# A two-layer backbone of four mixer groups on one core: the S5 group's TensorE steps given fixed places among the input projection's matmuls

## The chip, the cores and the metric

The kernel runs on one core of a Trainium2 chip, as one launch. The metric is device time in microseconds (us) of one execution; several executions are timed and the median is given. The core has five engines that run side by side, each through its own list of instructions in order: TensorE (PE, matmuls; PEld is its weight load), VectorE (DVE), ScalarE (ACT), GpSimd (POOL), and SyncE (SP), which issues DMA transfers. An instruction waits at the head of its engine's list until the data and buffers it needs are ready, and all behind it on that engine wait too.

## The reference

Two layers over 512 latent tokens and 256 context tokens, model width 2048. Each layer is one input projection that feeds four groups of heads, and one output projection:

```python
for l in range(DEPTH):                       # 2 layers
    z = modulated_rms_norm(x, c), modulated_rms_norm(ctx, c_ctx)
    s5, q, k, v, rkv, lora, hy, gate = split(z @ w_in[l])
    y_s5 = s5_mixer(s5, ...)                 # bidirectional complex state-space scan
    y_at = attn_mixer(q, k, v, ...)          # windowed attention with sink logits
    y_rw = rwkv_mixer(rkv, lora, ...)        # bidirectional RWKV-7 time mixing
    y_hy = hyena_seq(hy, ...)                # bidirectional order-2 long convolution
    y = concat(rms(y_s5), rms(y_at), y_rw, rms(y_hy))
    x = x + g * ((y * silu(gate)) @ w_out[l])

def s5_mixer(u):                             # 32 groups of 16 channels, 64 states, 2 directions
    h_t = lambda_bar * h_(t-1) + B_bar u_t   # associative scan, context first
    y = gelu(Re(C h) + d * u)
    return y * sigmoid(y @ glu_w + glu_b)
```

Layer 0 also produces the context's output; layer 1 needs only the latent one.

## The kernel before

**The input projection** is cut into tiles of 128 output columns. A tile takes its weights in four parts (loaded through `wr`, split into a high part `wh` on ACT, L1477, and a low part `wl` on DVE or POOL, L1478), and for each of 16 chunks of the input it runs three matmuls (L1638: high by high, high by low, low by high) 512 tokens wide, and three 256 wide where the context is computed. Three matmuls 512 wide are called a **unit** here, three 256 wide half a unit; a tile with the context is 24 units. L1535 and L1541 are matmuls of the next layer's modulation, which ride along with tiles.

**The order of a layer.** After the tile of the LORA columns come four tiles for S5 (`T_S5`), then the S5 group's own work; twelve tiles for RWKV (`T_R`); the RWKV group; then the projections of Q, K, V, of Hyena and of the gates, with attention, Hyena and the output projection (L1728) following. The code is written group by group, but a scheduler with a model of the engines decides at build time in which order the instructions of each engine stand. Matmuls of S5 so come to stand among those of the projection tiles that follow.

**S5** works on 16 batches (`batch`, four to each of four column tiles `tile`) in each layer. A tile loads u, transposes it twice on PE (L725, L733; evicted to `Uc` and `U`). A batch builds B on POOL and C on DVE and POOL (L768 to L779); `pk` is 16 small matmuls of C (L788), evicted to `kp`, written to memory and read back as the Toeplitz tile T by 16 transfers, whose two halves DVE adds (L805); `Bt` is four transposes (L811); `pv` is 16 matmuls of U (L831). From pv DVE and POOL make the state h (L833 to L849, scans at L839), and `py` is h by C (L855) and U by T (L857). A tile's readout transposes (L745) give y, which goes to memory; at the end comes the GLU over all four tiles (L880) and the group's rms norm, whose column sums are matmuls with ones at L134. After them the S5 buffers are given back, and the RWKV group's buffers take their place.

**RWKV** begins with features (L340 to L367, matmuls and transposes), which go by DMA to an inversion on POOL, L398 and L399 in turn; then a serial chain of steps (L446, L459, L439). Four columns by three blocks make 12 such blocks in a layer.

**Pace.** Units of the projections that run beside RWKV are held: a unit may not stand ahead of the RWKV step that its number asks for (`Pace`, with the first steps' allowance P0). These are order-only dependences: they fix who stands first in PE's list, and no engine waits on a semaphore for them.

**Milestones on PE.** Counted in units from the program's start, S5's first transposes of layer 0 stand at unit 67, its last norm matmuls at 317, the first feature matmul of RWKV at 360, the first chain step at 432, the third block's features at 474. In layer 1: 1296, 1494, 1524, 1604, 1638.

## Time and profile before

| | us |
|---|---|
| median of three runs | 3741.15 (3729.2 to 3751.39) |
| profiled execution | 3744.33 |
| its span | 3742.6 |
| PE busy in it | 3437.6 |
| DVE / ACT / POOL busy | 2169.5 / 1457.6 / 1305.2 |

The span is the time between the first and the last instruction on the core; the profiled execution's own time lies 1.7 us above it, and 3.2 us above the median. The mean granted TensorE clock is 0.942 of full speed. "Busy" counts matmuls and other work, not waiting. In rows of groups, "out<-in" names the tile written and those read.

### The profile page before, as it was taken

Reading aid. Unit: us, or ns where it says so; the run is one execution under the profiler, and the core shown is the slowest. Engines: PE = TensorE matmul, PEld = TensorE weight load, DVE = VectorE, ACT = ScalarE, POOL = GpSimd, SP = SyncE. Lnnn points to the kernel's source line nnn. Section 1 sums busy time; section 2 is a strip of 40 time slices with the busy share of each in tenths; the row PEclk is TensorE's granted clock in tenths of the full one; section 3 lists DMA queues with packets and bytes.
Section 4 is the critical chain, followed back from the end, with each engine's and each line's share of the span. In section 5 each row is a group of like instructions: output and inputs, shape, how many; then the busy total and the mean of one; then the engine's idle time right before and its main releaser. Section 6 shows DMA issues by size and latency. Waiting matters only on the chain. (4 is left out here: it accounts for less than half of the span.)

```text
span 3742.6 us, 63247 instructions
## 1 busy us (share of the span) xinstructions
PE 3437.6 (92%) x23478; PEld 2632.7 (70%) x23478; DVE 2169.5 (58%) x4011; ACT 1457.6 (39%) x2873; POOL 1305.2 (35%) x2328
## 2 busy tenths in 40 slices
PE   5998898999999999999999989778899989999999
PEld 1466676777777877787777776566776767677867
DVE  7675563546555553466668464754456565546765
ACT  3345443333433342345213454433334444435422
POOL 5654451244343432000144333631524355411031
PEclk9997999999999999999999989889998899899999
DMA  7854443644444444534533335444533334435244
GB/s 241 280 178 151 134 121 116 196 121 139 124 145 127 144 125 122 170 118 130 210 101 98 107 111 150 109 111 153 165 92 110 106 109 121 115 114 181 77 156 124
DMA packets 550608, 515.03 MB, mean 138 GB/s; under 512 B 166457, under 2 KB 396378, under 8 KB 549660
## 3 DMA queue, kind: packets, MB, share of 16 engines
q1 hardware_dynamic: 550300, 510.99, 45.0%
q8 instruction: 185, 3.03, 0.3%
q14 instruction: 123, 1.01, 0.1%
HBM read 404.40 MB, written 103.02 MB: 136 GB/s over the span
## 5 line engine op out<-in xcount | busy, mean ns | idle before, releaser
L1638 PE MATMUL pin<-hxh,wh 128*128 128x512 f32 (+1 forms) x2624 | 989.6, 377 | 19.6 <-ACT wh L1477 9.9
L1638 PE MATMUL pin<-hxh,wl 128*128 128x512 f32 (+1 forms) x2624 | 947.3, 364 | 9.6 <-POOL wl L1478 6.2
L1638 PE MATMUL pin<-hxl,wh 128*128 128x512 f32 (+1 forms) x2624 | 947.2, 362 | 0.0
L1477 ACT ACTIVATE wh<-wr 128x512 fp32r<-128x512 f32 x548 | 344.0, 629 | 861.0 <-PE pin L1638 426.9
L1638 PEld LDWEIGHTS pin<-hxh,wh 128*128 128x128 f32 x2624 | 507.7, 193 | 138.0 <-issue 34.3
L1638 PEld LDWEIGHTS pin<-hxh,wl 128*128 128x128 f32 x2624 | 506.5, 193 | 93.0 <-POOL wl L1478 8.5
L1638 PEld LDWEIGHTS pin<-hxl,wh 128*128 128x128 f32 x2624 | 508.7, 194 | 73.5 <-issue 5.6
L1478 DVE TENSOR_TENSOR wl<-wr,wh 128x512 fp32r<-128x512 f32 x434 | 319.4, 736 | 363.4 <-ACT wh L1477 345.4
L1478 POOL TENSOR_TENSOR wl<-wr,wh 128x512 fp32r<-128x512 f32 x114 | 155.0, 1360 | 927.0 <-ACT wh L1477 860.7
L398 POOL TENSOR_TENSOR rwtm<-rwAb,rwX 128x60 f32<-128x60 f32 (+24 forms) x744 | 257.7, 346 | 351.8 <-DMA rwAb<-rwAd 193.2
L399 POOL TENSOR_TENSOR rwX<-rwX,rwtm 128x60 f32<-128x60 f32 (+24 forms) x744 | 267.2, 359 | 57.2 <-DMA wr<-in_win 0.2
L1728 PE MATMUL pin<-yh,wl 128*128 128x512 f32 (+1 forms) x768 | 280.2, 366 | 5.7 <-DVE wl L1478 5.5
L1728 PE MATMUL pin<-yh,wh 128*128 128x512 f32 (+1 forms) x768 | 280.6, 367 | 2.9 <-ACT yh L1704 2.0
L1728 PE MATMUL pin<-yl,wh 128*128 128x512 f32 (+1 forms) x768 | 278.8, 363 | 2.2 <-DVE yl L1705 1.8
L1728 PEld LDWEIGHTS pin<-yh,wl 128*128 128x128 f32 x768 | 144.8, 189 | 32.1 <-DVE wl L1478 9.7
L1728 PEld LDWEIGHTS pin<-yh,wh 128*128 128x128 f32 x768 | 144.9, 189 | 28.8 <-ACT yh L1704 4.2
L1728 PEld LDWEIGHTS pin<-yl,wh 128*128 128x128 f32 x768 | 145.3, 189 | 25.8 <-DVE yl L1705 2.7
L1732 DVE SCALAR_TENSOR_TENSOR xt<-pin,GT,xt 128x512 f32<-128x512 f32 (+1 forms) x144 | 94.1, 656 | 95.7 <-PE pin L1728 95.3
L1535 PE MATMUL pin<-wr,cs 128*32 128x128 f32 x2048 | 115.9, 291 | 22.5 <-DMA wr<-in_wada 16.4
L448 ACT ACTIVATE rwKU<-mU 64x256 f32<-64x256 f32 x96 | 36.2, 377 | 173.9 <-PE mU L446 173.0
L405 ACT ACTIVATE rwXT<-rwXP 32x256 f32<-32x256 f32 x96 | 64.3, 670 | 81.6 <-DMA rwXP<-rwXd 80.1
L340 PE MATMUL mA<-rwZR,rwld 64*128 64x128 f32 x768 | 94.2, 292 | 1.4 <-DVE rwld L332 0.5
(606 smaller groups left out, 6204.6 us busy)
## 6 DMA issues: line engine op xcount, KB each, us to landing
wr<-in_win SPq DMA_DIRECT2D x408, 256.0 KB
wr<-in_wada SPq DMA_DIRECT2D x256, 256.0 KB
ada<-in_wada SPq DMA_DIRECT2D x64, 512.0 KB
wr<-in_wo SPq DMA_DIRECT2D x128, 256.0 KB
rwld<-rwF SPq DMA_DIRECT2D x20, 1024.0 KB
rwF<-ev SPq DMA_DIRECT2D x64, 256.0 KB
xt<-in_xin SPq DMA_DIRECT2D x32, 384.0 KB
rwLA<-ev SPq DMA_DIRECT2D x32, 384.0 KB
```

The costliest lines, as they stand in the source:

```text
L340: nc.tensor.matmul(pss[:, p, b, :], kb[hr, d * 2 + p, 2 * b:2 * b + 2, :].rearrange("p b s -> p (b s)"), ZR[hr, d, :, tt * 64:tt * 64 + 64 ...
L398: E.tensor_tensor(tm, Ab[:, 0:s, s:s + 1].to_broadcast([128, s, w]), X[:, s:s + 1, m:8].to_broadcast([128, s, w]), ALU.mult)
L399: E.tensor_tensor(X[:, 0:s, m:8], X[:, 0:s, m:8], tm, ALU.subtract)
L405: nc.scalar.activation(XT[r:r + 32, :, 32 * q:32 * q + 32].rearrange("p u (m g) -> p u m g", g=4), XR[r:r + 32].rearrange("p u (g m) -> p ...
L448: nc.scalar.activation(KU[rB, :, p, b, 1, :], up[rB].rearrange("p d a b -> p d (a b)"), AF.Copy, scale=-1.0)
L1477: nc.scalar.activation(h, raw, AF.Copy)
L1478: (nc.gpsimd if i % 4 == 3 else nc.vector).tensor_tensor(l, raw, h.bitcast(F32), ALU.subtract)
L1535: nc.tensor.matmul(ps[32 * j:32 * j + 32, :], self.cs[:, q * 4 + j, :], w3[:, j], start=q == 0, stop=q == 3, tile_position=(0, 32 * j))
L1638: mm.append(nc.tensor.matmul(ps, w[:, c], x[:, t], start=a, stop=b))
L1728: nc.tensor.matmul(ps, w[:, c], y[:, t], start=a, stop=b)
L1732: nc.vector.scalar_tensor_tensor(x[:, t], ps, self.GT[l][:, s, j:j + 1], x[:, t], ALU.mult, ALU.add)
```

## The change

A class `Weave` numbers the projection's units as they are issued, and takes S5's PE steps each with a place, in units. When it is closed, it lays a chain of order-only dependences through both lists: each step stands behind the last unit before its place, and each unit behind the last step before it. It covers the S5 tiles and the RWKV tiles of the projection (`T_S5`, `T_R`). With `S5AT` = (at, P), S5's first transposes stand at unit `at` of that count, batch pr has its place at b = at + 7 + pr·P: its B and C are issued for b − 1.05P, pk and Bt stand at b − 0.6P (batch 0 at `at` + 4), pv at b, py at b + 0.9P. A tile's transposes stand at 0.85P and 0.35P ahead of its first batch (tile 0 at `at` and `at` + 3), its readout 4.25P behind it.

So that code can be issued in that order, `tile` and `batch` become generators that name the place of their next piece, and `run` always takes the one with the lowest. U gets two buffers and the output columns `Yc` a tag of their own; small tiles share tags to make room. The GLU is issued last, as before, and is not given a place.

Line numbers shift: L1638 is L1699 after, L1535 L1596, L788 L833, L811 L856, L831 L878, L855 L904, L857 L906, L805 L850, L340 L374, L446 L480.

The diff, cut to its core:

```diff
+class Weave:
+    def unit(self, insts, w=1.0):
+        self.units.append((self.n, insts))
+        self.n += w
+    def step(self, at, insts):
+        self.steps.append((at, len(self.steps), insts))
+    def behind(self, insts, prev):
+        for i in insts:
+            self.tc.add_manual_dep(i.ins, prev.ins.name, mybir.DependencyInfo(mybir.DependencyClass.NoSync, mybir.DependencyReason.DATA), reason="weave")
+    def close(self):
+        self.steps.sort(key=lambda x: x[:2])
+        prev, step, q = None, None, list(self.steps)
+        for n, insts in self.units:
+            while q and q[0][0] <= n:
+                step = q.pop(0)[2]
+                if prev:
+                    self.behind(step, prev)
+                prev = step[-1]
+            if step:
+                self.behind(insts, step[-1])
+            prev = insts[-1]
...
 class S5:
...
+        yield b0 + (4 * ct - 0.85) * P if ct else self.at
...
-                nc.tensor.transpose(ps[0:96, i, :], u3[:, hf * 4 + i, :], idn)
+                self.lead(nc.tensor.transpose(ps[0:96, i, :], u3[:, hf * 4 + i, :], idn))
...
+        yield b0 + (4 * ct - 0.35) * P if ct else self.at + 3
-        U = t([128, 8, 128], "s5U")
+        U = t([128, 8, 128], "s5U", 2)
...
-        Yc = t([96, 8, 8, 16], "s5Uc")
-        for b in range(4):
-            self.batch(ct * 4 + b, U[:, b * 2:b * 2 + 2, :], Yc[:, :, b * 2:b * 2 + 2, :])
-        y = t([128, NT], "s5y")
+        Yc = self.Yc[ct] = t([96, 8, 8, 16], "s5Yc")
+        yield b0 + (4 * ct + 4.25) * P
+        y = t([128, NT], "s5u")
...
+    def lead(self, m):
+        self.weave.step(self.now, [m])
+
-    def batch(self, pr, U, Yc):
+    def batch(self, pr):
+        at, P = self.at + 7 + pr * self.per, self.per
+        yield at - 1.05 * P
...
+        yield at - 0.6 * P if pr else self.at + 4
         pk = k.bank("mA", 2, (128, 128))
...
+        yield at
         pv = k.bank("mU", 1, (128, 2, 2, 96))
...
+        yield at + 0.9 * P
         py = [k.bank("mY", 1, (128, 128))[0:96], k.bank("mI", 1, (128, 128))[0:96]]
...
     def run(self, srcs, outs, bg, eps):
         self.prepare()
-        for ct in range(4):
-            self.tile(ct, srcs[ct])
+        todo = [((b0 + (4 * ct - 2) * P, ct), self.tile(ct, srcs[ct])) for ct in range(4)]
+        todo += [((b0 + (pr - 1.06) * P, 4 + pr), self.batch(pr)) for pr in range(16)]
+        heap = {g: x for x, g in todo}
+        while heap:
+            g = min(heap, key=heap.get)
+            self.now = heap[g][0]
+            n = next(g, None)
...
         self.glu(outs, bg, eps)
...
                 if self.pace:
                     self.pace.unit(mm)
+                if self.weave:
+                    self.weave.unit(mm, (t.stop - t.start) / 512)
...
+S5AT = [(36, 19), (10, 17)]
```

What the two builds' lists hold. First PE, in layer 0, about one batch of S5 (mA takes pk and Bt, mU pv, mY and mI py). Before:

```order
L788 MATMUL mA_3547<-s5C_3538,s5BA_2770 32x128 x4
L788 MATMUL mA_3547<-s5C_3538,s5BB_2771 32x128 x2
L855 MATMUL mY_3515<-s5C_3428,s5h_3506 96x128
...
L855 MATMUL mI_3516<-s5C_3428,s5h_3506 96x128
L788 MATMUL mA_3547<-s5C_3538,s5BB_2771 32x128 x2
L811 MATMUL mA_3581<-c_ident,s5B_3529 128x128 x4
...
L857 MATMUL mY_3515<-s5T_3452,s5U_3294 96x128
...
L831 MATMUL mU_3598<-s5U_3294,s5Bt_3580 64x96 x8
L788 MATMUL mA_3657<-s5C_3648,s5BA_2770 32x128 x4
```

and after:

```order
L833 MATMUL mA_3645<-s5C_3607,s5BA_2770 32x128 x4
L833 MATMUL mA_3645<-s5C_3607,s5BB_2771 32x128 x4
L856 MATMUL mA_3679<-c_ident,s5B_3598 128x128 x4
L1596 MATMUL pin_5190<-wr_5307,cs 32x128 x4
L1699 MATMUL pin_5191<-hxh_1827,wh_5303 128x512
...
L1699 MATMUL pin_5356<-hxh_1507,wl_5397 128x512
L904 MATMUL mY_3696<-s5C_3497,s5h_3636 96x128
...
L906 MATMUL mY_3696<-s5T_3548,s5U_3335 96x128
L906 MATMUL mI_3697<-s5T_3548,s5U_3335 96x128
L1699 MATMUL pin_5356<-hxh_1515,wh_5396 128x512
...
L878 MATMUL mU_3728<-s5U_3335,s5Bt_3678 64x96 x8
```

Before, the py of an older batch (s5h_3506) stands in the middle of a younger batch's pk (mA_3547), with U by T (L857) some units later; after, pk and Bt stand together, then some nine units, then the older batch's py with its U by T, and two units on the younger batch's pv.

DVE at the same kind of place, where s5v and s5w carry a batch from pv to h, and wl is the low part of the projection's weights (L1478, after L1539; L259 is another split). Before:

```order
L805 TENSOR_TENSOR s5T_2968<-s5T_2968 128x256
L833 TENSOR_TENSOR s5v_3123<-mU_3114,s5cs_3109 128x384
L834 TENSOR_TENSOR s5w_3124<-mU_3114,s5sn_3108 128x384
L259 TENSOR_TENSOR wl_2442<-wr_2440,wl_2442 64x512
L795 SCALAR_TENSOR_TENSOR s5kp_3072<-s5eye_2699,s5dd_2698,s5kp_3072 64x16
L835 TENSOR_TENSOR s5v_3123<-s5v_3123,s5w_3124 128x384
L259 TENSOR_TENSOR wl_2447<-wr_2445,wl_2447 64x256
L839 SCALAR_TENSOR_TENSOR s5w_3124<-s5r_763_2710,s5v_3123 128x96 x4
L846 TENSOR_TENSOR s5v_3123<-s5w_3124,s5cs_3109 128x384
L833 TENSOR_TENSOR s5v_3233<-mU_3224,s5cs_3219 128x384
```

and after:

```order
L823 TENSOR_TENSOR s5C_3607<-s5C_3607,s5tm_3608 128x288
L823 TENSOR_TENSOR s5C_3607<-s5tm_3612,s5C_3607 128x288
L850 TENSOR_TENSOR s5T_3548<-s5T_3548 128x256
L880 TENSOR_TENSOR s5v_3627<-mU_3618,s5cs_3579 128x384
L881 TENSOR_TENSOR s5w_3628<-mU_3618,s5sn_3578 128x384
L882 TENSOR_TENSOR s5v_3627<-s5v_3627,s5w_3628 128x384
L886 SCALAR_TENSOR_TENSOR s5w_3628<-s5r_763_2710,s5v_3627 128x96 x4
L893 TENSOR_TENSOR s5v_3627<-s5w_3628,s5cs_3579 128x384
L894 TENSOR_TENSOR s5h_3636<-s5v_3627,s5hx_3639 128x2x64
L895 TENSOR_TENSOR s5h_3636<-s5v_3627,s5hx_3639 128x2x31
L896 TENSOR_TENSOR s5h_3636<-s5v_3627,s5hx_3639 128x2x95
L1539 TENSOR_TENSOR wl_5361<-wr_5358,wh_5360 128x512
```

Before, the addition of T stands ahead of the chain from pv, and the work of other batches and splits of weights stand within that chain; after, C of the next batch and the addition of T still stand ahead of it, the chain from pv to h stands in one piece, and the next split of weights behind it.

PE at the start of RWKV in layer 0 (L340, after L374, is the first feature matmul; mU from rwBV, L480, the chain's first step). Before:

```order
L1638 MATMUL pin_6550<-hxh_1827,wl_6662 128x256
L340 MATMUL mA_6947<-rwZR_6912,rwld_6915 128x128 x2
L340 MATMUL mA_6953<-rwZR_6912,rwld_6915 128x128 x4
L340 MATMUL mA_6959<-rwZR_6912,rwld_6915 128x128 x4
L351 MATMUL mA_6967<-c_ident,rwL_6920 128x128
...
L365 MATMUL mA_6999<-rwKU_6911,rwS_6910 64x64 x10
L1535 MATMUL pin_6732<-wr_6741,cs 32x128 x4
L1638 MATMUL pin_6733<-hxh_784,wh_6737 128x512
```

and after:

```order
L1596 MATMUL pin_11808<-wr_11853,cs 32x128 x4
L374 MATMUL mA_6941<-rwZR_6912,rwld_6915 128x128 x4
...
L385 MATMUL mA_6967<-c_ident,rwL_6920 128x128
...
L399 MATMUL mA_6999<-rwKU_6911,rwS_6910 64x64 x16
L374 MATMUL mA_7296<-rwZR_7267,rwld_7270 128x128 x4
...
L399 MATMUL mA_7354<-rwKU_7266,rwS_7265 64x64 x16
L449 MATMUL mI_7130<-rwXP_7021,rwS_6910 64x32 x16
L455 MATMUL mI_7150<-rwXT_1494_6904,rwXP_7021 32x32 x16
L480 MATMUL mU_7171<-rwBV_6914,rwXT_1494_6904 64x64 x4
L1699 MATMUL pin_11653<-hxh_1663,wh_11728 128x256
```

Before, units stand between the first half of block 1's features and what follows; after, both blocks' features and the chain's first step (L480) stand one after another with no unit between them.

In units: in layer 0, S5's first transposes stand at unit 60 now, its last batch ends at 376, the last norm matmuls (L134) stand at 424, RWKV's features of blocks 1 and 2 and the first chain step all at 448.5, the third block's features at 480. In layer 1: 1282, 1566, 1588, 1621, and 1640. From the third block on the lists stand alike again. Between the old and the new place of the last norm matmuls lie, beside the units, 17 groups of four modulation matmuls (L1535, now L1596) in layer 0, and 16 in layer 1.

## Rows read from the trace of the kernel before

**Rows 1.** Windows: length, busy us of PE, PEld, DVE, ACT, POOL, then clock, DMA, GB/s

```profile
270.00:593.00 323.00, 281.69 (x2185) 219.68 (x2183) 190.91 (x358) 140.10 (x292) 152.87 (x215) 0.90 0.47 136
593.00:665.00 72.00, 58.37 (x279) 40.12 (x280) 24.84 (x28) 21.30 (x38) 11.14 (x13) 0.88 0.36 116
840.00:1400.00 560.00, 541.60 (x4652) 433.62 (x4652) 314.25 (x629) 221.40 (x441) 216.31 (x575) 0.97 0.47 134
2211.00:2523.00 312.00, 253.89 (x1970) 195.23 (x1969) 184.93 (x345) 132.46 (x278) 138.71 (x195) 0.87 0.45 128
2523.00:2561.00 38.00, 37.31 (x166) 22.63 (x164) 12.41 (x19) 15.04 (x24) 7.06 (x7) 0.91 0.50 166
2746.00:3230.00 484.00, 449.72 (x3193) 333.39 (x3193) 280.87 (x566) 201.18 (x394) 228.49 (x569) 0.90 0.38 110
```

**Rows 2.** What PE waited for, 2205 to 2524 us: total, times, longest

```profile
PE mY L855 <- DVE s5h L848: 21.0, 7, 5.9
PE mY L857 <- DVE s5T L805: 8.9, 6, 2.9
```

**Rows 3.** One tile's instructions (s5Bt): duration ns least/median/most, first and last start

```profile
L831 PE MATMUL mU<-s5U,s5Bt x512: 246/246/423, 285.1 to 2507.7; 128*64 128x96 f32 x171
```

**Rows 4.** The chain of waits, one piece: start, us, what

```profile
3340.41 13.63 PE pin L1638 x58
```

**Rows 5.** The page's groups of instructions: the modulation matmuls

```profile
L1535 PE MATMUL pin<-wr,cs 128*32 128x128 f32 x2048 | 115.9, 291 | 22.5 <-DMA wr<-in_wada 16.4
```

**Rows 6.** Lines L134, L340, L446 in either layer: duration, first and last start

```profile
L134 PE MATMUL mA<-s5T,c_ones x2: 379/379/379, 664.1 to 664.3; 128*128 128x256 f32 x2
...
L134 PE MATMUL mU<-s5T,c_ones x2: 592/592/592, 2560.2 to 2560.6; 128*128 128x512 f32 x2
...
L340 PE MATMUL mA<-rwZR,rwld x103: 272/272/373, 700.5 to 899.9; 64*128 64x128 f32 x103
...
L340 PE MATMUL mA<-rwZR,rwld x96: 272/272/579, 2602.5 to 2753.7; 64*128 64x128 f32 x96
...
L446 PE MATMUL mU<-rwBV,rwXT x64: 218/218/267, 789.4 to 878.5; 64*64 64x64 f32 x64
...
L446 PE MATMUL mU<-rwBV,rwXT x40: 218/218/267, 2700.6 to 2747.7; 64*64 64x64 f32 x40
```

**Rows 7.** Timeline, start of RWKV: start, us, engine, line, tiles [idle before <-releaser]

```profile
692.08 0.68 DVE L332 TENSOR_TENSOR rwld<-rwL,rwla 128x512 f32<-128x512 f32 x1
...
720.95 1.17 PE L340 MATMUL mA<-rwZR,rwld 64*128 64x128 f32 x12
...
733.78 0.26 POOL L398 TENSOR_TENSOR rwtm<-rwAb,rwX 128x31 f32<-128x31 f32 x1 [6.34 <-DMA rwAb<-rwAd]
...
766.91 0.20 POOL L399 TENSOR_TENSOR rwX<-rwX,rwtm 128x8 f32<-128x8 f32 x1
...
839.71 0.71 PE L340 MATMUL mA<-rwZR,rwld 64*128 64x128 f32 x4
...
2745.85 0.93 PE L340 MATMUL mA<-rwZR,rwld 64*128 64x128 f32 x6
```

**Rows 8.** Timeline, S5 in layer 0: pk to T's addition twice, pv to h

```profile
279.51 0.40 PE L788 MATMUL mA<-s5C,s5BB 64*32 64x128 f32 x8
...
285.13 1.55 PE L831 MATMUL mU<-s5U,s5Bt 128*64 128x96 f32 x16
...
293.67 0.89 DVE L849 TENSOR_TENSOR s5h<-s5v,s5hx 128x190 f32<-128x190 f32 x1
...
304.58 0.43 DVE L805 TENSOR_TENSOR s5T<-s5T 128x256 f32<-128x256 f32 x1 [2.98 <-DMA s5KD<-s5kp]
...
391.94 0.40 PE L788 MATMUL mA<-s5C,s5BB 64*32 64x128 f32 x8
...
407.34 0.41 DVE L805 TENSOR_TENSOR s5T<-s5T 128x256 f32<-128x256 f32 x1
```

**Rows 9.** One tile's instructions (s5C): duration ns least/median/most, first and last start

```profile
L777 DVE TENSOR_TENSOR s5C<-s5CS,s5PR x32: 424/456/1544, 265.0 to 2494.7; 128x288 f32<-128x288 f32 x32
```

More of the change, by code (lines that the diff above doesn't have):

```diff
@@ L163, in unit, with __init__ @@
                 self.tc.add_manual_dep(i.ins, self.steps[self.at - 1][1], mybir.DependencyInfo(mybir.DependencyClass.NoSync, mybir.DependencyReason.DATA), reason="pace")
+class Weave:
+    def __init__(self, tc):
+        self.tc, self.units, self.steps, self.n = tc, [], [], 0.0
+    def unit(self, insts, w=1.0):
[18 more added lines that the diff above has]
+            prev = insts[-1]
+        for _, _, step in q:
+            self.behind(step, prev)
+            prev = step[-1]
 LWP = 0
@@ L595, with __init__ @@
 class S5:
-    def __init__(self, k, pool, l, ctx_out):
+    def __init__(self, k, pool, l, ctx_out, weave, at, per):
+        self.weave, self.at, self.per = weave, at, per
         self.k, self.nc, self.p, self.l, self.co = k, k.nc, pool, l, ctx_out
@@ L610, in prepare @@
         nc, k, t, V = self.nc, self.k, self.t, self.nc.vector
-        lam = t([128, 3, 32], "s5lam")
+        lam = t([128, 3, 32], "s5hx")
         nc.sync.dma_start(out=lam, in_=k.ins["s5lam"][self.l])
@@ L652, in prepare @@
         V.tensor_tensor(PI[:, :, 1], mag, sn, ALU.mult)
-        tq = t([128, 32, 4], "s5tq")
+        tq = t([128, 32, 4], "s5kp")
         for m in (1, 2, 4):
@@ L717, in tile @@
         N = NT if self.co else NL
+        b0, P = self.at + 7, self.per
         u = t([128, NT], "s5u")
         nc.sync.dma_start(out=u, in_=src)
+        yield b0 + (4 * ct - 0.85) * P if ct else self.at
         u3 = u.rearrange("p (c s) -> p s c", s=8)
@@ L787, in batch @@
                     a = (d * 16 + pr) * 16
-                    nc.tensor.matmul(pk[o:o + 32], Xf[r, a:a + 32], c[r, d, 0:8, :].rearrange("p j o -> p (j o)"), start=i == 0, stop=i == 1,
-                                     tile_position=(r.start, o))
+                    self.lead(nc.tensor.matmul(pk[o:o + 32], Xf[r, a:a + 32], c[r, d, 0:8, :].rearrange("p j o -> p (j o)"), start=i == 0, stop=i == 1,
+                                               tile_position=(r.start, o)))
         kp = t([128, 128], "s5kp", 1)
@@ L824, in batch @@
         cb = cs.unsqueeze(2).to_broadcast(sh)
+        yield at
+        U = self.U[pr // 4][:, pr % 4 * 2:pr % 4 * 2 + 2, :]
         pv = k.bank("mU", 1, (128, 2, 2, 96))
@@ L830, in batch @@
                     rhs = U[:, g, 0:96] if d == 0 else U[:, g, 32:128][:, ::-1]
-                    nc.tensor.matmul(pv[r, d, i, :], Bt[:, d, i, r], rhs, start=True, stop=True, tile_position=(0, r.start))
+                    self.lead(nc.tensor.matmul(pv[r, d, i, :], Bt[:, d, i, r], rhs, start=True, stop=True, tile_position=(0, r.start)))
         vr, vx = t(sh, "s5v", 2), t(sh, "s5w", 2)
@@ L849, in batch @@
         V.tensor_tensor(h[:, 1, :, 0:95][:, :, ::-1], vr[:, 1, :, 0:95], hx[:, 1, :, 0:95], ALU.add)
+        yield at + 0.9 * P
+        Yc = self.Yc[pr // 4][:, :, pr % 4 * 2:pr % 4 * 2 + 2, :]
         py = [k.bank("mY", 1, (128, 128))[0:96], k.bank("mI", 1, (128, 128))[0:96]]
@@ L854, in batch @@
                     c = C[r, i, d, 1:9] if d == 0 else C[r, i, d, 8:0:-1]
-                    nc.tensor.matmul(py[g], h[r, d, i], c, start=d + i == 0, stop=False, tile_position=(r.start, 0))
+                    self.lead(nc.tensor.matmul(py[g], h[r, d, i], c, start=d + i == 0, stop=False, tile_position=(r.start, 0)))
         for g in range(2):
-            nc.tensor.matmul(py[g], U[:, g, 32:128], T[:, 0, g, :], start=False, stop=True)
+            self.lead(nc.tensor.matmul(py[g], U[:, g, 32:128], T[:, 0, g, :], start=False, stop=True))
         for g in range(2):
@@ L869, in glu @@
             gw += [w[:, 0], w[:, 1]]
-        for kc, tag in enumerate(("s5u", "s5U", "s5Uc", "s5Bt")):
+        for kc, tag in enumerate(("s5u", "s5Yc", "s5Uc", "s5Bt")):
             y = t([128, NT], tag)
@@ L895, in run @@
         self.prepare()
-        for ct in range(4):
-            self.tile(ct, srcs[ct])
+        self.U, self.Yc = {}, {}
+        b0, P = self.at + 7, self.per
+        todo = [((b0 + (4 * ct - 2) * P, ct), self.tile(ct, srcs[ct])) for ct in range(4)]
[5 more added lines that the diff above has]
+            n = next(g, None)
+            if n is None:
+                del heap[g]
+            else:
+                assert n >= self.now, (n, self.now)
+                heap[g] = n, heap[g][1]
         self.glu(outs, bg, eps)
@@ L1467, in __init__ @@
         self.nc.vector.memset(k.eps4, 4e-6)
-        self.pace = None
+        self.pace = self.weave = None
     def raw(self, pool=None):
@@ L1750, in layer @@
         rw, u5 = self.rw, self.u5
+        self.weave = Weave(tc)
         for c in range(4):
@@ L1756, in layer @@
         with tc.tile_pool(name=f"s5{l}", bufs=1) as pool:
-            S5(k, pool, l, co).run(u5, y_s5, bg[0], self.eps)
+            S5(k, pool, l, co, self.weave, *S5AT[l]).run(u5, y_s5, bg[0], self.eps)
         for i, j in enumerate(a * 4 + c for c in range(4) for a in range(3)):
@@ L1763, in layer @@
             pass
+        self.weave.close()
+        self.weave = None
         with tc.tile_pool(name=f"rw{l}", bufs=1) as pool:
```

8 lines of the change are left out of this document (5 added, 3 removed).

## The prediction, made before the changed kernel ran

> **What bounds the kernel now.** The order of reading is windows by stage, then PE's waits, then the places at which one group hands over to the next. In the RWKV stage of layer 0 PE is busy 541.60 of 560 us at a granted clock of 0.97; in S5's stage it is busy 281.69 of 323 and 58.37 of 72 us in layer 0, 253.89 of 312 and 37.31 of 38 in layer 1, at clocks of 0.87 to 0.91 [rows 1]. So PE's own list bounds the kernel, and S5's stages are where that list stands still. Idle there comes to 54.9 us (layer 0) and 58.8 us (layer 1). A clock below 1 is a share of time at the lower level (1.2 instead of 2.4 GHz): 0.90 is one fifth of the time. The same pv matmul takes 246 ns or 423 ns [rows 3], so busy time at the lower level is 42% lost: 0.2 × 281.69 × 0.42 + 0.24 × 58.37 × 0.42 = 30 us in layer 0, 0.26 × 253.89 × 0.42 + 0.18 × 37.31 × 0.42 = 31 us in layer 1. Together 85 and 90 us of slack. The largest named waits in layer 1 are py waiting for h (21.0 us in 7) and U by T waiting for T's addition (8.9 us in 6) [rows 2]: chains PE → DVE → PE that PE reached too early.
>
> **The change part by part.** Nothing is computed that was not computed before, so all that counts is where PE's list waits. I follow it to two points: R, the last norm matmuls of S5 (664.1 and 2560.2 us before [rows 6]), whose end frees the buffers RWKV needs, and the third RWKV block's features (839.71 and 2745.85 [rows 7]), from which on both lists stand alike.
>
> *Up to R.* After the change 107 more units stand ahead of R in layer 0, 94 more in layer 1. Fifty-eight projection matmuls in a row took 13.63 us [rows 4], 0.235 each, 0.705 a unit: 75 and 66 us. The 17 and 16 groups of modulation matmuls between come with 115.9 / 2048 × 8 = 0.45 us each (a group of four in the list is eight in the trace) [rows 5]: 8 and 7 us. These units are not extra work; they are done later before, and come back below.
>
> What the slack of S5's stage becomes, x, no row shows, since S5 never ran so. The nearest from below is the RWKV stage of layer 0, also a chain with units laid out beside it: idle 18.4 us and clock loss 0.06 × 541.6 × 0.42 = 13.6, together 32 on 528 of plain work, 6%. From above the same stage of layer 1: idle 34.3 and 0.2 × 449.7 × 0.42 = 37.8, 72 on 412, 17.5% [rows 1]. The plain work up to R is 395 − 85 + 83 = 393 us and 350 − 90 + 73 = 333 us, so x is 24 to 69 in layer 0 and 20 to 58 in layer 1. I take the middle, 46 and 39: the pv and py places have room (below), but the first tile, the readouts and the GLU have none laid out. R then falls at 664 + 83 − 85 + 46 = 708, and 2560 + 73 − 90 + 39 = 2582.
>
> Why x can lie below the old slack: from pk to pv the list now holds 0.6P units, 11.4 in layer 0, some 8 us, and about 5 us of S5's own matmuls; from pv to py 0.9P, 12 us and about 3. From pv's end (285.13 + 1.55) to the end of h (293.67 + 0.89) it took 7.9 us [rows 8]; in the list after, that chain stands on DVE in one piece. So py has some 7 us to spare. T's addition, which stands ahead of that chain on DVE, came 15.4 us after pk ended in the third tile (391.94 + 0.40 to 407.34), and 24.7 us in the first (279.51 + 0.40 to 304.58) [rows 8]. With 15.4 it holds up pv's DVE work by some 2 us, which the 7 cover.
>
> The price of moving B and C earlier, of U's second buffer and of the new tags is nothing on PE: their work on DVE and POOL is the same. Behind the T addition on DVE queue pv's chain and then the next weight split (wl), for which the projection's units wait; that cover is the 7 us again, and what it costs without is a rival below.
>
> *From R on.* Before, R to features took 36 us (664.5 to 700.5) and 41 us (2561 to 2602.5) [rows 6]; the features' last input on DVE (L332) was done at 692.76 [rows 7], so 28 us is a floor in layer 0. I take 30 and 33. The units that fill this are in the list after (24.5 and 33).
>
> Features to the first chain step took 89 and 98 us [rows 6], with units between that PE had to do first. After, both blocks' features and the first chain step stand together with no unit between, so PE waits for the chain alone. Its parts in block 1 of layer 0 [rows 7]: from the second half of the features (720.95) to POOL's start at 733.78, 13 us, held by a DMA; POOL's inversion 733.78 to 767.11, 33 us with other work of POOL in it, about 25 by the steps of 0.35 us that fill most of it; then 22 us to 789.4, some 17 without the units between. An estimate of 55 us, the floor about 50, the ceiling 68 (720.95 to 789.4). [...]
>
> First chain step to the third block's features: before 50.3 us with 42 units (30 us) in layer 0, 45.3 us with 34 units (24 us) in layer 1 [rows 6, 7], so 21 us besides. After, 31.5 units (22 us) and 18 (13 us): 43 and 34 us.
>
> *The sum.* Layer 0: 708 + 30 + 55 + 5 + 43 = 841, against 839.7, but six units (4 us) further on: a gain of 3. Layer 1: 2582 + 33 + 55 + 5 + 34 = 2709 against 2745.9, one unit further on: a gain of 38. Together 41. The profiled execution took 3744.3 us, so 3703; it lies 3.2 above the median of the runs, so 3700.
>
> **The rivals.**
>
> *Dense S5 stage.* x is at its lower bounds, 24 and 20: 41 us more, 3659. For it: the waits of [rows 2] are just those that the places take away. Against it: the first tile's batches, and DVE and POOL. The trace shows DVE and POOL busy 190.91 + 152.87 = 344 us in a window of 323 [rows 1], so they do run side by side, but C's multiplication took from 424 to 1544 ns [rows 9], so at times one holds up the other. The Trainium skill, page "SBUF — State Buffer", section "SBUF: two separate sides", says that the two share a port pair as "an exclusive lock, not a bandwidth split", the loser blocked for a whole instruction. By that rule alone, with no overlap at all, layer 1 would have 185 + 139 + 12 + 7 = 343 us of both before R, R not before 2554 without the added splits, so a dense stage there would be all but excluded; the 344 in 323 us say that it does not hold for every pair of instructions, and I lower this case only a little for it.
>
> *RWKV's start isn't shortened.* From R to the first chain step it stays at 125 and 139 us as before [rows 6], because that time is the chain's (DMA, POOL) and not the units'. Then the 107 and 94 units that stood there before are gone and PE idles: 35 and 46 us worse than forecast, 3781. It decides above a mean of 112 us from R to the first chain step, where the change stops paying. Against it: of the 125 us before, 115 units (81 us) were PE's own work, of the 139 us 110 units (78 us). A start shortened by only half gives 3740, no change.
>
> *T comes late.* This ends on the other side. If T needs 24.7 us after pk in every batch, as in the first tile [rows 8], its addition holds pv's chain up by 24.7 − 13 = 12 us where 7 are covered, and py and the next wl split behind it come 5 us late, in all 32 batches: 160 us, of which x already holds the 41 above its lower bounds. That gives 3700 + 119 = 3819. From a mean of 22.6 us after pk the change costs more than it gains (41 + 41 = 82 over 32 batches is 2.6 each). Against it: from the second tile on it took 15.4, and sixteen small transfers to a batch are the same as before.
>
> *The places do nothing*, because the scheduler had much the same order: excluded, since R stands 107 and 94 units later in the list.
>
> **How the numbers follow.** The forecast has a chance of 0.50, with a range of its own of 3675 to 3725 by x; the dense stage 0.16; a start only half shortened, no change, 0.17; not shortened at all 0.10; T late 0.07. About 0.5% of the time, 19 us, is what a measurement of this kernel can tell from no change, so faster means below 3722. Of the forecast's chance about 0.46 lies there, and all of the dense stage's: 0.62. Within 0.5% lie the half-shortened start and 0.04 of the forecast, 0.21. Slower: 0.17. The range goes from 3642 (17 us below the dense stage) to 3765, which leaves out T late, most of the start that isn't shortened, and little below.
>
> **What would show it.** After, PE busy over span between S5's first transposes and R should be near 0.9 at a clock above 0.92 (x); the waits of py for h (L904 for L894 to L896) should be gone, and T's addition (L850) should come 14 to 18 us behind pk. R should stand near 708 and 2582 us, RWKV's first chain step (L480) some 90 us behind it, with one hole on PE of about 40 us, waiting for rwXT, in each layer. The third block's features should stand near 841 and 2709. The prediction is wrong if R lies beyond 740 or 2615, if R to the first chain step takes over 112 us, or if the gain sits anywhere behind the third block.

## The result: 3.75% slower, and the profile after

The changed kernel took 3877.5 us (3865.1 to 3896.3) against 3737.2 for the kernel before in the same comparison: ratio 1.0375, 95% interval 1.0318 to 1.0433. The forecast was 3700. The profiled execution has a span of 3863.4 us; TensorE is busy 3434.4 of it, within 4 us of before. So all of the loss is time in which its list stands still, 124 us more than before in the two profiles.

The lines of the profile after at the points to which the sum was worked out, as in [rows 6] (R, the first features, the first chain step, in either layer):

```profile
L134 PE MATMUL mA<-s5T,c_ones x2: 378/378/379, 791.8 to 792.0; 128*128 128x256 f32 x2
...
L134 PE MATMUL mU<-s5T,c_ones x2: 591/592/592, 2760.2 to 2760.6; 128*128 128x512 f32 x2
...
L374 PE MATMUL mA<-rwZR,rwld x128: 272/417/579, 821.9 to 987.4; 64*128 64x128 f32 x128
...
L374 PE MATMUL mA<-rwZR,rwld x160: 272/272/579, 2789.3 to 2990.5; 64*128 64x128 f32 x160
...
L480 PE MATMUL mU<-rwBV,rwXT x72: 218/218/336, 880.1 to 995.4; 64*64 64x64 f32 x72
...
L480 PE MATMUL mU<-rwBV,rwXT x104: 218/218/366, 2847.2 to 2998.2; 64*64 64x64 f32 x104
```

and the third block's features, which answer to the last two of [rows 7]:

```profile
922.80 0.93 PE L374 MATMUL mA<-rwZR,rwld 64*128 64x128 f32 x7
...
2878.11 1.04 PE L374 MATMUL mA<-rwZR,rwld 64*128 64x128 f32 x7
```

R came at 792, not 708. From there on the steps are those of the forecast: 30 us to the features (forecast 30), 58 to the first chain step (55), 43 to the third block (43 and 5 for the clock). Layer 1 begins 93 us late (layer 0's last norm matmuls start at 2099.0 instead of 2005.9); taken off, R stands at 2667, not 2582, and then come 29, 58 and 31 us (forecast 33, 55, 34 and 5). Both layers went wrong by 84 or 85 us up to R. Less goes on behind the third block: layer 0 loses some 14 us more there before layer 1 begins, and layer 1 wins some 10 back before its end.

Windows of the profile after (columns as in [rows 1]); the first and the last but one are units 60 to 130 and 1282 to 1343, in which S5's first batches run beside the LORA matmuls:

```profile
268.50:416.00 147.50, 98.00 (x621) 72.15 (x622) 50.95 (x106) 57.99 (x108) 50.19 (x73) 0.76 0.44 132
416.00:792.00 376.00, 324.84 (x2440) 252.57 (x2439) 168.86 (x313) 138.38 (x268) 127.02 (x180) 0.95 0.43 126
792.00:822.00 30.00, 23.71 (x166) 17.77 (x164) 21.74 (x38) 9.73 (x17) 3.08 (x7) 0.90 0.74 239
822.00:880.00 58.00, 25.59 (x216) 21.39 (x216) 21.96 (x48) 14.28 (x36) 25.97 (x76) 0.50 0.31 89
880.00:922.80 42.80, 41.88 (x348) 33.54 (x348) 17.71 (x41) 14.00 (x27) 16.31 (x50) 0.91 0.25 63
2302.00:2404.00 102.00, 80.31 (x558) 60.66 (x558) 41.15 (x84) 46.32 (x90) 32.98 (x48) 0.82 0.44 138
2404.00:2760.60 356.60, 292.33 (x2140) 218.80 (x2139) 164.57 (x317) 142.09 (x268) 120.97 (x170) 0.91 0.45 130
```

The same units 60 to 130 before the change, for the first of these:

```profile
265.70:386.50 120.80, 101.14 (x650) 76.80 (x649) 60.40 (x111) 60.14 (x115) 55.17 (x79) 0.82 0.53 162
```

Idle there was 20 us and is 50. The hole at RWKV's start is much as forecast (about 40 us): 32 us of 58 idle, the clock at 0.50, its lower level, throughout.

What TensorE waited for in layer 0's S5 stage, 260 to 792 us (total, times, longest):

```profile
PE pin L269 <- ACT ev L266: 26.4, 3, 11.7
PE pin L1596 <- DMA wr<-in_wada: 18.4, 13, 6.7
PE pin L300 <- DVE wl L293: 17.9, 6, 7.0
PE pin L300 <- ACT ev L301: 17.1, 5, 5.6
```

The waits of py for h and T, which the change aimed at, are gone. In their place stand waits of matmuls that have no place in the chain: the RWKV feed's norm (L269), LORA's products (L300) and the modulation (L1596). The same waits were there before, but shorter (260 to 665 us; L235 is L269 after, L266 is L300, L1535 is L1596):

```profile
PE pin L235 <- ACT ev L232: 13.8, 2, 9.8
...
PE pin L266 <- ACT ev L267: 4.0, 3, 3.0
...
PE pin L1535 <- DMA wr<-in_wada: 3.6, 3, 1.8
PE pin L266 <- DVE wl L259: 2.2, 1, 2.2
```

The chain of waits shows one way in which such a wait comes about (layer 1; start, us, what):

```profile
2392.25 0.28 ACT s5kp L839
...
2392.55 7.16 DMA s5KD<-s5kp
...
2402.02 3.99 DMA wr<-rwlz
...
2407.84 1.83 DMA s5T<-s5KD
...
2409.69 0.43 DVE s5T L850
2410.11 1.02 DVE s5w L886 x4
...
2411.20 1.38 POOL s5hx L892
...
2412.61 0.62 ACT s5sn L866 x2
...
2418.48 0.70 ACT ev L301
...
2419.22 1.53 PE pin L300 x3
```

pk's result goes to memory and comes back through SyncE's list, with a LORA load (rwlz) between; VectorE's addition of T holds pv's chain; GpSimd's hx follows; the next batch's sine on ScalarE waits for hx; and behind the sine stands the eviction for which LORA's matmul waits. VectorE's waits at that addition in layer 0's stage have grown, after (270 to 792 us), then before (270 to 665, two rows):

```profile
DVE s5T L850 <- DMA s5T<-s5KD: 61.5, 16, 10.9
```

```profile
DVE s5T L805 <- DMA s5T<-s5KD: 8.4, 5, 4.0
DVE s5T L805 <- DMA s5KD<-s5kp: 8.2, 2, 5.2
```

The sine's wait for hx is not new, it was longer before; so this piece shows one path and not how much of the loss goes by it (same windows, after, then before):

```profile
ACT s5sn L866 <- POOL s5hx L892: 26.0, 9, 6.2
```

```profile
ACT s5sn L821 <- POOL s5hx L845: 38.1, 12, 5.3
```

### The profile page after: what moved, and what is told of

It reads as the page before. It is cut to its first block, busy times and chain, and to the rows that moved or that the text cites. A ratio compares the mean times of both kernels' runs of the same rounds, so it can differ in the third digit from the quotient of the medians.

```text
span 3863.4 us, 63115 instructions
## 1 busy us (share of the span) xinstructions
PE 3434.4 (89%) x23478; PEld 2623.5 (68%) x23478; DVE 2122.1 (55%) x4011; ACT 1478.9 (38%) x2889; POOL 1302.5 (34%) x2328
## 5 line engine op out<-in xcount | busy, mean ns | idle before, releaser
L1699 PE MATMUL pin<-hxh,wh 128*128 128x512 f32 (+1 forms) x2624 | 997.5, 380 | 11.5 <-ACT wh L1538 6.1
L1699 PE MATMUL pin<-hxh,wl 128*128 128x512 f32 (+1 forms) x2624 | 943.4, 361 | 6.3 <-POOL wl L1539 4.5
L1699 PE MATMUL pin<-hxl,wh 128*128 128x512 f32 (+1 forms) x2624 | 946.2, 361 | 0.0
L1699 PEld LDWEIGHTS pin<-hxh,wh 128*128 128x128 f32 x2624 | 509.2, 194 | 127.9 <-issue 32.1
L1699 PEld LDWEIGHTS pin<-hxh,wl 128*128 128x128 f32 x2624 | 508.0, 194 | 87.9 <-POOL wl L1539 6.7
L1699 PEld LDWEIGHTS pin<-hxl,wh 128*128 128x128 f32 x2624 | 510.6, 195 | 68.4 <-issue 4.7
L1539 DVE TENSOR_TENSOR wl<-wr,wh 128x512 fp32r<-128x512 f32 x434 | 321.9, 742 | 319.8 <-ACT wh L1538 289.7
L1539 POOL TENSOR_TENSOR wl<-wr,wh 128x512 fp32r<-128x512 f32 x114 | 154.1, 1352 | 857.2 <-ACT wh L1538 721.4
L432 POOL TENSOR_TENSOR rwtm<-rwAb,rwX 128x60 f32<-128x60 f32 (+24 forms) x744 | 268.9, 361 | 347.0 <-DMA rwAb<-rwAd 182.0
L1596 PE MATMUL pin<-wr,cs 128*32 128x128 f32 x2048 | 123.3, 295 | 45.2 <-DMA wr<-in_wada 40.3
L374 PE MATMUL mA<-rwZR,rwld 64*128 64x128 f32 x768 | 106.0, 319 | 37.1 <-DVE rwld L366 31.1
L374 PEld LDWEIGHTS mA<-rwZR,rwld 64*128 64x128 f32 x768 | 91.3, 215 | 52.9 <-issue 36.4
```

Of the source, the lines that this page charges most:

```text
L374: nc.tensor.matmul(pss[:, p, b, :], kb[hr, d * 2 + p, 2 * b:2 * b + 2, :].rearrange("p b s -> p (b s)"), ZR[hr, d, :, tt * 64:tt * 64 + 64 ...
L432: E.tensor_tensor(tm, Ab[:, 0:s, s:s + 1].to_broadcast([128, s, w]), X[:, s:s + 1, m:8].to_broadcast([128, s, w]), ALU.mult)
L1539: (nc.gpsimd if i % 4 == 3 else nc.vector).tensor_tensor(l, raw, h.bitcast(F32), ALU.subtract)
L1596: nc.tensor.matmul(ps[32 * j:32 * j + 32, :], self.cs[:, q * 4 + j, :], w3[:, j], start=q == 0, stop=q == 3, tile_position=(0, 32 * j))
L1699: mm.append(nc.tensor.matmul(ps, w[:, c], x[:, t], start=a, stop=b))
```

## The experiments

Theories. A: T's round trip, by the chain above. B: SyncE's row of 16 loads keeps weight loads back. C: the places take S5's steps away from the ends of projection tiles, where L269 and L300 then wait with nothing before them. D (of the two runs that leave matmuls out): TensorE would wait there whatever stands. E, formed after the second set: the late end of S5 costs, not the places. Ratios are to the kernel before, with 95% intervals.

**T's addition behind h** (`t_last`).

```diff
-        V.tensor_tensor(T[:, 0], T[:, 0], T[:, 1], ALU.add)   # ahead of pv
+        tl = V.tensor_tensor(T[:, 0], T[:, 0], T[:, 1], ALU.add)   # behind h, whose last part is hl
+        self.weave.behind([tl], hl)
```

> The changed kernel with one order-only dependence more: on VectorE the addition of T's halves (L850) stands behind the last part of h instead of ahead of pv's chain. Theory A (T's round trip through memory, some 16 us after pk, holds the addition; behind it wait pv's chain, GpSimd's hx, the next batch's sine on ScalarE and, behind that, the projection's evictions and the RWKV feed): the waits of the feed's norm matmuls (L269, 26 and 29 us) and of the LORA matmuls (L300, 35 and 28 us) halve, TensorE's idle in S5's stages falls from 97 and 84 to about 65 and 55 us, time about 3815. Theory B (SyncE's 16 loads in a row keep weight loads back) and theory C (S5's small matmuls no longer fill the gaps where the feed's and LORA matmuls wait): those waits stay, time 3863 to 3893.

3844.6, ratio 1.0305 (1.0256 to 1.0353): 33 us, about half of what A alone would give. Idle up to R was 86 and 73 us, not 65 and 55, and the waits of L269 and L300, which A expected to halve, fell only from 118 to 100 us (whole program). A is a part at most.

**T by 4 transfers** (`t_four`).

```diff
-            for s in range(8):
...
-                nc.sync.dma_start(out=T[s * 16:s * 16 + 16, d], in_=KT[d, 0:16, :, of:of + 128])
+            for g in range(2):   # one pattern whose 8 pieces overlap, 16 columns apart
+                src = KT[d, 0:16, g, 16 * (1 - d):16 * (1 - d) + 128]
+                src = bass.AP(src.tensor, src.offset, [[16, 8]] + [list(x) for x in src.ap])
+                nc.sync.dma_start(out=T[:, d, g], in_=src)
```

> The changed kernel with T read back by 4 transfers in place of 16 (the same bytes and rows, overlapping reads in one pattern). SyncE's 7.3 us of issuing per batch becomes about 2. Theory A: T's addition comes some 5 us earlier, just ahead of pv's end, and the waits behind it go: time about 3815, idle of S5's stages about 65 and 55 us. Theory B: the waits of the modulation matmuls for wr (18 and 15 us) go as well or alone: 3840 if alone. Theory C: 3863 to 3893.

3833.7, ratio 1.0278 (1.0237 to 1.0319). From pk's end to T's addition a mean of 10.9 us in layer 0, after 16.7 (mean over its 16 batches, from the trace). The wait of the modulation matmuls in layer 0's stage, 18.4 above, is all but gone, and L269 waits on (270 to 775 us):

```profile
PE pin L269 <- ACT ev L266: 27.0, 3, 11.2
...
PE pin L1597 <- DMA wr<-in_wada: 0.9, 1, 0.9
```

In layer 1's stage it hardly fell, from 14.5 to 11.0 us (2180 to 2760 us):

```profile
PE pin L1597 <- DMA wr<-in_wada: 11.0, 6, 4.3
```

VectorE's wait at T's addition did not fall with the earlier addition (61.5 us above; 270 to 775 us here), so it is no measure of what A costs:

```profile
DVE s5T L851 <- DMA s5T<-s5KD: 80.6, 15, 10.3
```

So B is real in layer 0, and this edit, which bears on A and B together, gives back no more than a third of the loss (44 us).

**No chain of places** (`no_weave`).

```diff
     def close(self):
+        return
```

> The changed kernel with the streams, the buffers and the issue order, but without the chain of places: the scheduler sets S5's steps among the units itself. S5 then ends early in the list (last norm at unit 229 and 1403, before the change 317 and 1494). Theory C: S5's steps fill the gaps again, time near before, 3730 to 3790. Theories A and B: the round trips of T stand closer together, py waits for h and T as before the change and more, while all units stay for later: S5's stages alone cost 100 us idle in each layer or more; time 3780 to 3880.

3740.2, ratio 1.0032 (1.0007 to 1.0056), in C's range. The streams and buffers cost next to nothing; the chain of places costs the rest. But S5 also ends early in this list, so C was not yet told from E.

**More units ahead of the first chain step** (`p0`).

```diff
-P0 = [20, 0]
+P0 = [60, 40]
```

> The changed kernel with P0 = [60, 40] in place of [20, 0]: 40 more groups of three matmuls may stand ahead of RWKV's first chain step, 30 units in layer 0, 30 in layer 1. All theories leave S5's stages as they are. If the holes between the features and the first chain step (58 us each, half of it idle, the clock at 0.50) are time lost, they fill: time about 3830. If the chain is what counts from there on, the units moved ahead are missed later: 3863 to 3893.

3843.6, ratio 1.0304 (1.0262 to 1.0347): 34 us, where filling both holes promised some 50. R and the first chain step stand where they stood (793 and 883 us in layer 0); the units put between fill the hole in part (idle from R to the first chain step 22 us, 39 after the change), and some of it comes back behind: 7 us of idle up to the third block, where the kernel after has 1.

**LORA's and the feed norm's matmuls left out**, after and before (`after_bare`, `before_bare`).

```diff
-                nc.tensor.matmul(ps[:, :n], self.k.c["blk1"], sq[:, a:a + n], start=True, stop=True)
-                nc.scalar.activation(sq[:, a:a + n], ps[:, :n], AF.Sqrt, ...)
+                nc.scalar.activation(sq[:, a:a + n], sq[:, a:a + n], AF.Sqrt, scale=64.0, ...)
...
-                    nc.tensor.matmul(ps, ws[:, c * 128:c * 128 + 128], xs, start=True, stop=True)
-                    nc.scalar.activation(st[:, a:a + n], ps, AF.Tanh, ...)
+                    nc.scalar.activation(st[:, a:a + n], xs, AF.Tanh, ...)
```

> The changed kernel without the matmuls of the RWKV feed's norm (L269) and of LORA (L300): the square root and the tanh behind them read their inputs directly (this part of the computation is left out). Everything else on TensorE keeps its place. Theory C (places take S5's steps away from the ends of projection tiles, where TensorE then waits for these two): their waits, 118 us in all, go, and little else grows: time 3760 to 3790, and the difference to the kernel before with the same matmuls left out is 50 to 80 us (the two holes at RWKV's start and T's part). Rival D (TensorE waits there for the evictions of the banks, whatever stands at a tile's end): the wait goes over to the next units; time above 3825, the difference stays above 110.

> The kernel before without the same matmuls (the feed's norm, L235, and LORA, L266; this part of the computation is left out). Theory C: their waits there are some 40 us: time 3690 to 3715. Rival D: 3715 to 3737.

3840.2 and 3702.3: the difference is 138 us, as it is with these matmuls in (140). The kernel after came out as D says; the kernel before by itself fell in C's range (3690 to 3715). C, as the wait of these two matmuls, fell as the main cause. The wait went over to the modulation matmuls, up to 23.6 us at a time (whole program; 40.3 us in all in the kernel after):

```profile
PE pin L1592 <- DMA wr<-in_wada: 123.6, 31, 23.6
```

**Places as an upper bound only** (`steps_free`): in `close`, a step stands behind the step before it, not behind the units.

```diff
-                step = q.pop(0)[2]
-                if prev:
-                    self.behind(step, prev)
-                prev = step[-1]
+                s = q.pop(0)[2]
+                if step:
+                    self.behind(s, step[-1])
+                step = s
...
```

> The changed kernel with half of the chain of places: units still stand behind the S5 steps whose place has come, and the steps keep their order, but a step no longer waits for the units ahead of its place, so that it may come earlier. Its list has the last norm at units 264 and 1443 and units between RWKV's features and the first chain step. Theory C: steps stand at tile ends again, waits of L269 and L300 under 40 us in all, time 3720 to 3750. Theory A alone: T's waits are as in the run without the chain; the same. If the places by themselves cost nothing and only the late end of S5 does: 3760 to 3800.

3746.5, ratio 1.0037 (1.0009 to 1.0066): S5 runs ahead of its places and the loss is gone. This is in the range of C and A, below that of the late end (3760 to 3800); but S5 ends early in this list as well, so it parts them no better than `no_weave`.

**No chain, T by 4 transfers** (`nw_four`): the edits of `no_weave` and `t_four`.

> The run without the chain of places, and T read back by 4 transfers in place of 16. There py waited 18.6 us for T's addition and 30.7 us for h: the first goes, part of the second too, so 3740 becomes 3715 to 3725, below the kernel before. If T isn't what comes last: 3735 to 3745.

3705.3, ratio 0.9926 (0.9893 to 0.9959): faster than the kernel before, and 10 us below the range.

**Closer places** (`p_small`), with R and the features at the units of the kernel before.

```diff
-S5AT = [(36, 19), (10, 17)]
+S5AT = [(36, 13), (10, 11)]
```

> The changed kernel with S5AT = [(36, 13), (10, 11)]: the places stand closer, so that S5's last norm matmuls stand at units 317 and 1494 and RWKV's features at 360 and 1525, as before the change. If places at fixed distances themselves cost (theory C, and A by its stalls in each batch), S5's stages keep an idle of 85 to 100 us in each layer, and only the holes at RWKV's start (some 55 us together) go: time 3810 to 3830. Theory E (the late end costs: S5 is stretched over more tiles, and no units are left for RWKV's start): S5's idle is 50 to 60 us in each layer, time 3720 to 3750.

3754.3, ratio 1.0054 (1.0032 to 1.0077). This tells the most: a chain of places that stand closer, with S5 ending where it ended before the change, takes back 123 of 140 us. It is 4 us above E's range, and S5's idle is 80 and 58 us, not 50 to 60: E holds for most of the loss, as long as T comes by 16 loads; the run doesn't part the earlier end from the closer places that bring it about. Idle is left above all in units 60 to 130, 44 us against 20 before:

```profile
266.70:414.80 148.10, 104.26 (x723) 77.19 (x723) 62.55 (x127) 71.96 (x132) 64.22 (x93) 0.79 0.46 137
```

From R to the first chain step TensorE is idle 9 and 22 us; the kernel after had 39 (above) and 34 there. The lines are layer 0 and layer 1 here, then layer 1 after (the profile here is of an execution 17 us above the median):

```profile
686.80:811.50 124.70, 115.65 (x832) 92.95 (x830) 57.51 (x96) 44.57 (x86) 47.77 (x114) 0.93 0.60 187
2582.30:2720.70 138.40, 115.98 (x818) 92.16 (x816) 66.97 (x101) 52.10 (x94) 53.92 (x129) 0.89 0.52 160
```

```profile
2761.20:2847.20 86.00, 51.50 (x397) 41.41 (x396) 41.32 (x80) 25.47 (x55) 30.79 (x86) 0.68 0.46 140
```

**Both matmuls left out and T by 4 transfers** (`four_bare`), at the old places: the edits of `after_bare` and `t_four`.

> The changed kernel with T read back by 4 transfers and without the matmuls of the feed's norm and of LORA (that part of the computation is left out), at the old places (19 and 17 units). If T's loads on SyncE and TensorE's waits at tile ends are the two sources, each covering for the other when one alone is taken away, S5's idle falls to 30 to 45 us in each layer and the time to 3750 to 3780. If a third thing holds TensorE, idle stays above 60 in each layer and the time is 3795 to 3835.

3810.0: idle up to R 76 and 69 us, as forecast for a third thing that holds TensorE, most of it in units 60 to 130 in layer 0 (53 us).

**T by 4 transfers in the kernel before** (`before_four`): the edit of `t_four`.

> The kernel before with T read back by 4 transfers. If SyncE's row of 16 loads keeps weight loads back in every order, some 20 to 30 us go: 3705 to 3715. If it only does so with the places: 3725 to 3740.

3687.5, ratio 0.9865 (0.9823 to 0.9908). The 16 loads cost without any places too, and more than forecast.

**Closer places and T by 4 transfers** (`four_small`): the edits of `p_small` and `t_four`.

> The changed kernel with both: closer places (13 and 11 units) and T by 4 transfers. Theory E: below the kernel before, 3695 to 3715. If places themselves cost: 3765 to 3790.

3771.0, ratio 1.0097 (1.0066 to 1.0127): a miss for E, in the range of places that cost by themselves, and 17 us above the closer places alone. Units 60 to 130 are idle 42 us in it, and 1282 to 1343 32 us; why it is above `p_small` stays open. Against `before_four`, which has the same T and R near the same units (312 and 1511, here 317 and 1494), it is 83 us slower, and nearly all of that lies in S5's stages: idle up to R 82 and 67 us here, 31 and 38 there (layer 0, layer 1; here, then `before_four`):

```profile
271.50:693.30 421.80, 339.49 (x2485) 256.27 (x2486) 202.24 (x386) 169.31 (x333) 159.00 (x228) 0.87 0.41 124
2239.70:2602.00 362.30, 295.20 (x2191) 218.01 (x2192) 183.82 (x367) 153.56 (x309) 141.09 (x203) 0.87 0.43 129
```

```profile
270.60:634.50 363.90, 332.81 (x2420) 254.97 (x2418) 207.01 (x377) 152.51 (x319) 163.12 (x225) 0.91 0.45 139
2203.50:2535.40 331.90, 293.99 (x2215) 222.93 (x2214) 188.86 (x366) 148.28 (x307) 146.61 (x203) 0.92 0.48 144
```

With T by 4 transfers the late end is thus 63 us (3833.7 to 3771.0), and 83 us stay with the places. The waits of L269 and L300 show the same over the whole program: 118 us in the kernel after, 101 in `p_small` and 104 here, against 34 in the kernel before, 26 in `before_four` and 17 in `no_weave`. They go with the places and not with the late end.

**Steps moved to tile ends** (`snap_four`): the edit of `t_four`, and a place less than 8 units ahead of an end of a tile with L269 or L300 behind it becomes that end.

```diff
     def step(self, at, insts):
+        for e in self.ends:          # (48, 72, 96, 144, 216, 288, 360) in layer 0
+            if e - 8 < at < e:
+                at = e
```

> Against the run with T by 4 transfers (3834): each S5 step whose place lies up to 8 units ahead of the end of a tile with LORA or feed-norm matmuls behind it stands at that end instead, just ahead of them. Theory C (bare tile ends): the waits of L269 and L300 (27 and 34 us in layer 0) fall to under 15 and 25, time 3800 to 3815. If the S5 steps are too short to cover (2 to 3 us against waits of 7 to 11), 3825 to 3840.

3825.5 against 3833.7: the intervals of both ratios overlap. The waits of L269 and L300 in layer 0 fell to 20 us each (262 to 790 us), where C had under 15 and under 25. Bare tile ends are at most a small part.

**S5 behind LORA** (`late_four`): the edit of `t_four`, and places that begin later and end where they did.

```diff
-S5AT = [(36, 19), (10, 17)]
+S5AT = [(98, 15), (72, 13)]
```

> Against the run with T by 4 transfers (3834): S5AT = [(98, 15), (72, 13)], so that S5 begins behind the three tiles with LORA matmuls (units 72 to 120 and 1296 to 1344), its last batch ending where it did. If S5's first batches and LORA's loads and splits hold each other up in the lists of SyncE, VectorE and ScalarE, TensorE's idle in units 60 to 130 falls from 41 to under 20 us and in 1282 to 1343 from 21 to about 12, and the time to 3795 to 3810. If LORA's matmuls wait because nothing stands beside them, idle there stays above 35 and the time is 3825 to 3850.

3795.6, ratio 1.0156 (1.0118 to 1.0195): 38 us less than `t_four`, as forecast for a collision. Units 60 to 130, first in `t_four`, then here:

```profile
268.70:407.40 138.70, 98.05 (x622) 72.15 (x622) 52.01 (x106) 58.03 (x108) 50.01 (x73) 0.78 0.46 140
```

```profile
266.30:369.20 102.90, 82.25 (x462) 61.88 (x461) 25.67 (x42) 36.21 (x70) 23.56 (x33) 0.80 0.58 179
```

Idle fell from 41 to 21 us, though LORA's matmuls now stand barer than before. The places also stand closer here (15 and 13 units), which this run doesn't part from the later start; but over the whole program idle fell by 20 us, no more than these units give. The other 15 us between the two profiles are less busy time.

**The kernel before, T by 4 transfers and without the addition** (`before_none`).

```diff
-        V.tensor_tensor(T[:, 0], T[:, 0], T[:, 1], ALU.add)
...
-            nc.tensor.matmul(py[g], U[:, g, 32:128], T[:, 0, g, :], start=False, stop=True)
+            for d in range(2):
+                nc.tensor.matmul(py[g], U[:, g, 32:128], T[:, d, g, :], start=False, stop=d == 1)
```

> The kernel before with T read back by 4 transfers (3688 so), and with its two halves given to TensorE apart (two more matmuls of U by T per batch and group of states) in place of VectorE's addition. If VectorE's waiting at the addition still holds work behind it there, 3665 to 3680; if the 4 transfers took all of that away, 3683 to 3695.

3665.1, ratio 0.9799 (0.9768 to 0.9831), the fastest version of the study.

**Places kept, the causes taken away** (`tight_none`): the edits of `t_four` and `before_none` in the changed kernel, and `S5AT = [(98, 11), (72, 9)]`.

> The changed kernel with the places kept and what the runs found taken away together: S5 begins behind LORA's tiles and its places stand closer (S5AT = [(98, 11), (72, 9)], last norm at units 352 and 1519), T by 4 transfers and its halves given to TensorE apart. If S5's early start beside LORA, T's round trip and the late end of S5 are what the change cost, nothing is left against the kernel before with the same T (3665): 3660 to 3690. If fixed places cost by themselves, it stays above 3715.

3681.5, ratio 0.9859 (0.9831 to 0.9886). Places that begin behind LORA's tiles cost little, 16 us against `before_none`, which has the same T (the intervals of the two ratios touch); they gain nothing.

## Why the prediction was wrong

Its failed step is one term, x, "what the slack of S5's stage becomes": 46 and 39 us were put there, where R at 792 and 2667 gives 130 and 124. With the right x the sum would have been 3872, for a profiled execution of 3865. What the runs showed in its place is idle time: up to R TensorE was idle 97 and 84 us after the change, 55 and 59 before. The loss by the clock, worked out as the prediction does it, was 33 and 34 us, and 30 and 31 before. So the slack of S5's stages, which was to fall from 175 to 85 us over both layers, grew to 254, and R lay beyond the limits that the prediction had set for itself (740 and 2615).

- *The bounds of x came from stages that share only TensorE's picture.* The RWKV stages have laid-out units too, but no LORA loads and no 16 transfers per batch in SyncE's list. S5's waits were read at TensorE alone ([rows 2]). Those waits did go, and others, which end on SyncE's transfers, VectorE and ScalarE, took more than their place. That the old ones had covered the new ones is argued, not shown.
- *T's addition was followed as far as py and the next weight split, no further.* It was 16.7 us behind pk in layer 0 (15.4 taken, and 22.6 as the point from which it decides), so the rival of T coming late did not decide in the form it had. The 15.4 was one batch, the fifth and so of the second tile (15.0 from pk's end, by [rows 8]); before the change the batches from the second tile on had a mean of 17.7 in layer 0, and all 16 one of 21.7. What stood behind the addition was not named to the end: pv's chain, hx, the sine, and then the projection's evictions. A and B together are worth some 40 us (`t_last`, `t_four`).
- *The first batches beside LORA were counted as if they were any others.* TensorE's idle beside them is 30 us more than before in layer 0 and 10 in layer 1; 38 us came back when S5 began behind LORA, with closer places (`late_four`).
- *Stretching S5 was priced only at its units.* While S5 runs with T by 16 loads, its stage stays idle, however it is ordered: up to R 55 and 59 us before ([rows 1]), 54 and 63 in `no_weave` with R at units 229 and 1403, 80 and 58 in `p_small`, 97 and 84 after. (The profiles of `no_weave` and `p_small` are of executions 18 and 17 us above their medians.) At the length of before, places gained nothing; with 107 and 94 units more the idle was greater still. And the moved units were then missing at RWKV's start, where the two holes, forecast rightly, were to be paid for by a gain in S5 that never came.
- *A small term without a run:* no run shows the 5 us of clock behind the hole as such. In layer 0 the clock after the change was at 0.91 over the 42.8 us from the chain's start to the third block, which is an estimate of 3 us (0.18 × 41.88 × 0.42).
- *Right:* R to the features, features to the chain's start, the way to the third block; the hole itself; py's waits gone. The change did what it says, and the rival in which RWKV's start isn't shortened did not happen (88 us from R to the first chain step, not 125).
- *Not settled:* the three causes overlap, since `t_four`, `late_four` and `p_small` take back more together than was lost; their shares can't be added. With T by 16 loads the late end of S5 matters most (`p_small`, 123 us). By the two profiles its gain is shared out evenly: from the kernel after to `p_small`, idle up to R falls by 42 us over both layers and idle from R to the first chain step by 42. With T by 4 loads the late end is 63 us, and places that begin beside LORA cost 83 (`four_small` against `before_four`). Why these two stay so far apart, when `p_small` and the kernel before differ by 18, is open.

## What to carry to other kernels

A wait read at the busiest engine names the last link only: before pinning that engine's steps, follow each of its waits back through the in-order lists of the others, and name what shares those lists. When work is spread over a longer stretch to hide its latency, ask what had been filling the stretch behind it. Here the gain lay in the latency itself: fewer transfers and one addition less in the kernel before (2.0% faster) beat every order of places that was tried.

## What the hardware showed beyond that

SyncE took 7.3 us to issue T's 16 loads one behind the other, 0.46 us each, and nothing else of its list went out in that time (the kernel after, SyncE's list; start, us):

```profile
450.27 7.31 SPq L849 DMA_DIRECT2D s5T<-s5KD  x16
457.68 0.40 SPq L1594 DMA_DIRECT2D wr<-in_wada  x1
```

The Trainium skill, page "DMA: Bandwidth & Descriptors", section "Anatomy of one DMA — SWDGE (gpsimd) path", says that the DMA engines do not wait on semaphores, the issuing sequencer does. The trace agrees: T's loads waited for the stores of kp at the head of SyncE's list, 26.2 us in 18 waits in layer 0's stage (270 to 792 us), and what stood behind them, such as wr above, went out behind them:

```profile
SPq L849 <- DMA s5KD<-s5kp: 26.2, 18, 5.7
```
